# The first norm of a hybrid block as a pipeline in program order

## The chip, the cores and the metric

The kernel runs on one core of a Trainium2 chip. A core has a matrix engine (TensorE, PE in the profile), a vector engine (VectorE, DVE), an activation engine (ScalarE, ACT), a general engine (GpSimd, POOL) and a sync engine (SyncE, SP), from whose queue this kernel starts all its transfers. The metric is the device time of one execution in microseconds; less is better. Before the change it was 1269.47 us, the median of three runs (1269.19 to 1269.53).

## The reference

One layer of an encoder on 1024 tokens and 16 meta tokens of width 1024, in float32. What matters here is its beginning:

```python
h = jnp.concatenate([meta, x], axis=1)
u = rmsnorm(h, norm_mix)            # h * rsqrt(mean(h*h) + 1e-6) * norm_mix
z = jnp.einsum('bld,dn->bln', u, w_in)
a, q, k, v, r, lr, ga, gb = jnp.split(z, IN_SPLITS, axis=-1)
```

From these eight parts a pooling mixer and a chunked gated linear attention are computed, merged by sigmoid gates, projected and added to h; a second norm, a squared-ReLU MLP (1024 to 4096 to 1024) and a last norm follow.

## The kernel before, in words

Every product is made in split precision: an operand is stored as a rounded high part and a low part that holds the rest, and a product is the sum of three (high by high, high by low, low by high). The high part is an ACT copy, the low part a subtraction on DVE or POOL.

The function `start` (lines 513 to 573) makes the first norm and turns the result. The tokens are eight tiles of 128 rows. For a tile t, `layer_norm` (221) sums the squares of each row on ACT (226), takes the inverse root with two small ACT and four small DVE instructions (`inv_sqrt`, 199), and scales by the root and by norm_mix on DVE (228); norm_mix lies on all 128 partitions in `gB`, put there by a transfer that repeats the row 128 times (537). `turned` (502) transposes the normed tile on PE in two groups of four into two PSUM banks, and copies each bank three times: the high part into `TH` (ACT, 196), the low part into `TL` (DVE, 197) and the plain value into `ut` (ACT, 511). Tiles 0 to 3 are the first token half, 4 to 7 the second.

`v_tile(0, t)` (456) multiplies the turned tile by 272 weight columns, 256 value columns and 16 of a low-rank gate, in 24 PE instructions into one bank. Two copies leave the bank: the 16 columns on DVE into `lrtok` (470), then the 256 on ACT into `v` (474). `load_vw` (441) loads and splits these weights. `lr_turn` (476) transposes lrtok.

`Quarters` (285) makes the gate projections by a Strassen-like scheme of seven products P1 to P7 per pair of weight blocks, each 12 PE instructions. P1 and P2 take the first token half as it is; P5, P6, P7 and P4 take sums and differences of the transposed halves, which `differences` (588) makes out of `ut` (lines 580, 581 and 586). `prime` (334) makes the first four weight operands, P1 and P2 of two pairs; each `next(run)` in `start` issues one product. P2 adds to P1's bank, but only once ACT has copied P1 out of it (360). P5 is the first product after `differences`.

What sets the order: PE's instructions are issued in the order of the code (1449). SP, ACT, DVE and POOL are ordered by a planner, which takes what it expects to be ready and prefers what stands earlier in the code. Each engine then works strictly through its list, and waits for semaphores where an input or a buffer isn't free. In the code the products P1 and P2 of the first pair and `v_tile` of tile 0 stand ahead of the norm of tile 4, `v_tile` of tiles 1 to 3 between the tiles 5 to 7, and `v_tile` of tiles 4 to 7 in `differences`, behind the meta tokens (`v_tile(0, 8)`, 572).

PSUM: two banks `mm` for the value products, four banks `ms` for the transpositions, one double bank `sc` for P1 and P2.

Of the kernel before, what the change touches and what calls it, by code (L numbers as in the profile page):

```python
# [14 lines left out]
P = 128  # L15
# [88 lines left out]
def kernel(  # L104
# [81 lines left out]
    def f32(ap):  # L186
        return ap.bitcast(F32)
# [32 lines left out]

    def layer_norm(xt, u):

        rows = xt.shape[0]
        ss = ln_stat[ln_n[0] % 4][:rows]
        ln_n[0] += 1
        act.activation(u, xt, ACT.Square, accum_out=ss)
        rs = inv_sqrt(ss, 1, 1.0 / D)
        dve.scalar_tensor_tensor(u, xt, rs, gB[:rows], ALU.mult, ALU.mult)

    turn_n = [0]  # L230

# [206 lines left out]
    def halves():  # L438
        return [slice(h * HALF, (h + 1) * HALF) for h in range(2)]

    def load_vw(i):
        vw, n = S["vw"][i], 256 + 16 * (i == 0)
        for j in range(2):
            r = raw.load(w_cols(C_V + i * 256 + j * P), D).rearrange("p (k c) -> p k c", k=KT)
            c = slice(j * P, (j + 1) * P)
            act.activation(vw[:, 0, :, c], r, ACT.Copy)
            eng = pool if i else dve
            eng.tensor_tensor(vw[:, 1, :, c], r, f32(vw[:, 0, :, c]), ALU.subtract)
        if i == 0:
            r = S["lrraw"]  # L450
            act.activation(vw[:, 0, :, 256:], r, ACT.Copy)
            pool.tensor_tensor(vw[:, 1, :, 256:], r, f32(vw[:, 0, :, 256:]), ALU.subtract)

    vm = gB[32 : 32 + META, : 2 * 256]

    def v_tile(i, t):

        vw, w = S["vw"][i], 256 + 16 * (i == 0)
        if t == 8:
            half, at, n = 0, 0, META  # L460
        else:
            half, n = t // 4, P
            at = OFF[half] + (t % 4) * P
        b = bank("mm")[:n, :w]
        mm3(
            b, KT, lambda k: (TH[half][:, k, at : at + n], TL[half][:, k, at : at + n]),
            lambda k: (vw[:, 0, k], vw[:, 1, k]),
        )
        if i == 0:
            dve.tensor_copy(S["lrtok"][:n, t], b[:, 256:])  # L470
        if t == 8:
            act.activation(vm[:, i * 256 : i * 256 + 256], b[:, :256], ACT.Copy)
        else:
            act.activation(S["v"][i][:, t], b[:, :256], ACT.Copy)

    def lr_turn():
        b = bank("ms")
# [21 lines left out]
        lambda i, w, b, u: gate_result(i, w, b, u),  # L499
    )  # L500

    def turned(u, t):

        half, at = t // 4, OFF[t // 4] + (t % 4) * P
        for j in range(2):
            b = quad(bank("ms"))
            for i in range(4):
                pe.transpose(b[:, i], u[:, (4 * j + i) * P : (4 * j + i + 1) * P], ident)
            k = slice(4 * j, 4 * j + 4)
            split_from_psum(TH[half][:, k, at : at + P], TL[half][:, k, at : at + P], b)  # L510
            act.activation(S["ut"][half, j][:, :, (t % 4) * P : (t % 4 + 1) * P], b, ACT.Copy)

    def start():
        act.preload_act_table_set("natural_log_exp_and_others")
# [18 lines left out]
        S["vw"] = [right.push("vw0", [P, 2, KT, VP], F32R)]  # L533
        load = lambda t: nc.sync.dma_start(xs[:, t % 4], x[t * P : (t + 1) * P, :])
        load(0)
        nc.sync.dma_start(ident, ident_in)
        nc.sync.dma_start(gB, bcast(norm_mix))
        for t in (1, 2, 3):
            load(t)
        q.load(0, 0)  # L540
        m = lambda half, j: tuple(a[half][:, 4 * j : 4 * j + 4, OFF[half] : OFF[half] + HALF] for a in (TH, TL))
        q.x.update({"P1": m(0, 0), "P2": m(0, 1), "P3": m(1, 1)})
        run = S["gate_run"] = q.run()
        for t in range(8):
            if t < 4:
                layer_norm(xs[:, t % 4], us[:, t % 3])
                turned(us[:, t % 3], t)
                load(t + 4)
                if t == 0:
                    nc.sync.dma_start(S["lrraw"], w_in[:, C_LR : C_LR + 16].rearrange("(k p) c -> p k c", p=P))  # L550
                    load_vw(0)
                    q.load(1, 0)
                continue
            if t == 4:
                nc.sync.dma_start(xm, meta)
                q.load(0, 1)
                q.load(1, 1)
                nc.sync.dma_start(mf, masks)
                q.prime()
                next(run)  # L560
                next(run)
                v_tile(0, 0)
            layer_norm(xs[:, t % 4], us[:, t % 3])
            turned(us[:, t % 3], t)
            if t < 7:
                v_tile(0, t - 3)
            else:
                layer_norm(xm, um)
        next(run)
        transposed(um, 0, 0)  # L570
        next(run)
        v_tile(0, 8)
        pool.tensor_copy(mask, mf)
# [14 lines left out]
    def differences():  # L588

        b11, b21, b12, b22 = (0, 0), (0, 1), (1, 0), (1, 1)  # L590
        left.pop_to(S["left_x"])
        differ(b11, b12, b11)
        halved("P5", b11)
        differ(b12, b22, b12)
        differ(b22, b22, b11)
        halved("P6", b22)
        for t in range(4, 8):
            v_tile(0, t)
        lr_turn()
        right.pop_to(S["right_ut"][4])  # L600
        halved("P7", b12)
        differ(b21, b21, b22)
        right.pop_to(S["right_ut"][2])
        halved("P4", b21)
        right.pop_to(S["right_ut"][0])
# [884 lines left out]
```

## Time and profile before

| | before |
|---|---|
| median of three runs | 1269.47 us |
| profiled execution | 1271.45 us |
| its span in the trace | 1269.7 us |
| VectorE busy | 853.2 us |
| ScalarE busy | 625.2 us |
| GpSimd busy | 60.3 us |

The profiled execution is one run under the profiler; its span goes from the first to the last instruction on the chip. All times within the trace count from the span's start. A row of the timeline gives the start, the duration, the engine, the line, the operation, what it writes and reads, how many like it follow each other (x), and in brackets how long its engine had been idle before it and what it then waited for.

### The profile page before, as it was taken

How to read it: one execution, taken by the hardware profiler on the slowest of the kernel's cores; microseconds unless marked ns; L12 is line 12 of the kernel's file. 1: busy time of each engine (PE TensorE's matmuls, PEld its weight loads, DVE VectorE, ACT ScalarE, POOL GpSimd, SP SyncE). 2: the span in 40 equal slices, each digit the busy share in tenths (PEclk: the TensorE clock that was granted, in tenths of full speed). 3: DMA queues.
4: the chain of work that ended last, by engine and by line, in shares of the span. 5: the costliest groups of instructions: out<-in, count | busy, mean ns of one | idle time of the engine just before them, and what ended most of it. 6: DMA issues, size and time to landing. Idle time of an engine off the chain costs nothing.

```text
span 1269.7 us, 18153 instructions
## 1 busy us (share of the span) xinstructions
PE 1221.4 (96%) x6799; PEld 1003.4 (79%) x6799; DVE 853.2 (67%) x1403; ACT 625.2 (49%) x1101; POOL 60.3 (5%) x38
## 2 busy tenths in 40 slices
PE   3999999999999999899999999999999999999997
PEld 2888888888787877788878888888878788888775
DVE  6776667563355766842797766766764877887685
ACT  7567757431344664421565554544553444445444
POOL 0000000001000114510000000000000000000000
PEclk9999999999999999999999999999999999999999
DMA  9023334327210326860234444444469863332422
GB/s 261 1 67 108 113 95 143 115 67 231 84 35 10 95 93 205 275 239 34 84 116 158 162 146 149 157 150 149 160 221 373 275 230 100 95 97 92 166 92 83
DMA packets 143864, 175.41 MB, mean 138 GB/s; under 512 B 11008, under 2 KB 83472, under 8 KB 143776
## 3 DMA queue, kind: packets, MB, share of 16 engines
q1 hardware_dynamic: 143776, 174.25, 42.3%
q8 instruction: 53, 0.87, 0.3%
q14 instruction: 35, 0.29, 0.1%
HBM read 120.74 MB, written 53.48 MB: 137 GB/s over the span
## 4 chain that ended last, share of the span: by engine, by line
PE 86%; DVE 5%; ACT 3%; DMA 3%; issue 2%; POOL 1%; SPq 0%; DVEq 0%; ACTq 0%; POOLq 0%
PE b_mm L252 8%; PE b_mm L254 8%; PE b_mm L253 8%; PE b_o L253 8%; PE b_o L254 8%; PE b_o L252 8%; PE b_y L252 5%; PE b_y L254 5%; PE b_y L253 5%; PE b_z L252 3%; PE b_sc L252 3%; PE b_z L253 3%; PE b_sc L253 3%; PE b_sc L254 3%; PE b_z L254 3%
## 5 line engine op out<-in xcount | busy, mean ns | idle before, releaser
L252 PE MATMUL b_mm<-th,w1h 128*128 128x512 f32 (+1 forms) x240 | 86.9, 362 | 0.9 <-ACT w1h L75 0.9
L254 PE MATMUL b_mm<-th,w1l 128*128 128x512 f32 (+1 forms) x240 | 84.5, 352 | 0.7 <-DVE w1l L76 0.7
L253 PE MATMUL b_mm<-tl,w1h 128*128 128x512 f32 (+1 forms) x240 | 84.6, 352 | 0.0
L270 ACT ACTIVATE w1h<-raw 128x512 fp32r<-128x512 f32 x96 | 59.6, 623 | 45.1 <-PE b_sc L253 14.2
L252 PE MATMUL b_sc<-th,w1h 128*128 128x512 f32 x192 | 77.1, 402 | 1.8 <-ACT u2p L360 1.8
L252 PE MATMUL b_o<-w1h 128*128 128x512 f32 x192 | 75.3, 392 | 2.7 <-DVE h L1298 1.7
L253 PE MATMUL b_sc<-tl,w1h 128*128 128x512 f32 x192 | 76.2, 397 | 0.3 <-DVE tl L197 0.3
L253 PE MATMUL b_o<-w1l,w1h 128*128 128x512 f32 x192 | 75.0, 391 | 1.2 <-DVE w1l L271 1.2
L254 PE MATMUL b_sc<-th,w1l 128*128 128x512 f32 x192 | 76.2, 397 | 0.0
L254 PE MATMUL b_o<-w1h,w1l 128*128 128x512 f32 x192 | 75.0, 391 | 0.1
L271 DVE TENSOR_TENSOR w1l<-raw,w1h 128x512 fp32r<-128x512 f32 x96 | 65.6, 684 | 12.4 <-ACT w1h L270 12.4
L270 ACT ACTIVATE w1h<-fs 128x512 fp32r<-128x512 f32 x72 | 45.4, 630 | 49.9 <-PE b_y L253 34.4
L252 PE MATMUL b_z<-th,w1h 128*128 128x512 f32 x160 | 62.5, 391 | 0.8 <-DVE c L612 0.8
L253 PE MATMUL b_z<-tl,w1h 128*128 128x512 f32 x160 | 62.4, 390 | 0.4 <-DVE tl L1210 0.4
L254 PE MATMUL b_z<-th,w1l 128*128 128x512 f32 x160 | 62.3, 389 | 0.0
L271 DVE TENSOR_TENSOR w1l<-fs,w1h 128x512 fp32r<-128x512 f32 x72 | 49.3, 685 | 17.5 <-ACT w1h L270 17.5
L270 ACT ACTIVATE w1h<-bt 128x512 fp32r<-128x512 f32 x45 | 28.3, 630 | 57.1 <-issue 33.5
L1361 DVE TENSOR_TENSOR bt<-w,w 128x512 f32<-128x512 f32 x80 | 54.7, 684 | 2.4 <-DMA w<-in_w_ff_dram 2.4
L252 PEld LDWEIGHTS b_mm<-th,w1h 128*128 128x128 f32 x240 | 45.8, 191 | 10.1 <-issue 2.3
L254 PEld LDWEIGHTS b_mm<-th,w1l 128*128 128x128 f32 x240 | 45.9, 191 | 7.0 <-DVE w1l L76 1.0
L253 PE MATMUL b_o<-fxl,fxh 128*128 128x512 f32 x128 | 50.0, 391 | 0.7 <-DVE small L213 0.7
L252 PE MATMUL b_mm<-wo,th 128*128 128x512 f32 x128 | 50.7, 396 | 0.0
(334 smaller groups left out, 3396.4 us busy)
## 6 DMA issues: line engine op xcount, KB each, us to landing
hf_dram<-h SPq DMA_DIRECT2D x112, 256.0 KB, 2.1
raw<-hf_dram SPq DMA_DIRECT2D x112, 256.0 KB, 2.6
w<-in_w_ff_dram SPq DMA_DIRECT2D x64, 256.0 KB, 5.1
raw<-in_w_in_dram SPq DMA_DIRECT2D x24, 512.0 KB, 4.6
raw<-in_w_ff_dram SPq DMA_DIRECT2D x16, 512.0 KB, 4.1
rawx<-in_w_ff_dram SPq DMA_DIRECT2D x16, 512.0 KB, 4.2
xs<-in_x_dram SPq DMA_DIRECT2D x8, 512.0 KB, 6.3
rawx<-in_w_in_dram SPq DMA_DIRECT2D x8, 512.0 KB, 4.5
```

The source lines that it names most:

```text
L252: pe.matmul(ps, ah, bh, start=first and i == 0, stop=False, skip_group_check=more)
L253: pe.matmul(ps, ah, bl, start=False, stop=False, skip_group_check=more)
L254: pe.matmul(ps, al, bh, start=False, stop=last and i == n - 1, skip_group_check=more)
L270: act.activation(hi, a, ACT.Copy)
L271: dve.tensor_tensor(lo, a, f32(hi), ALU.subtract)
L1361: dve.tensor_tensor(bt, w, S["w2"][q[3:]][:, i], ALU.add if q[2] == "+" else ALU.subtract)
```

## The change

`start` becomes a software pipeline. The loop of tile t first issues the norm and the transpositions of tile t + 1, then the copies out of the banks of tile t (`taken`), the copies of the values of tile t - 1 (`leave`), and the value product of tile t. Within this loop ACT and DVE keep the order of the code, like PE (`manual_schedule`). The three copies of a bank are redistributed: both high parts on ACT, both low parts on DVE, of the plain values one on ACT and one on DVE.

norm_mix is loaded as one row of 4 KB and spread by two PE products with a column of ones, one for each half of `gB`; two DVE copies bring it from PSUM to `gB`, behind the inverse root of tile 0 and ahead of its scaling. The value weights are loaded ahead of x tiles 2 and 3; one half of their low part moves from DVE to POOL, and the 16 columns' low part from POOL to DVE. `prime` moves into the loop, behind the values of tile 4. All value products of the eight tiles come in the loop; the P1 and P2 products of the first two pairs all come behind it, and the norm of the meta tokens too. `differences` loses its four value products.

```diff
--- before.py
+++ after.py
@@ -220,12 +220,17 @@
 
     def layer_norm(xt, u):
 
+        scaled(xt, u, inv_rms(xt, u))
+
+    def inv_rms(xt, u):
         rows = xt.shape[0]
         ss = ln_stat[ln_n[0] % 4][:rows]
         ln_n[0] += 1
         act.activation(u, xt, ACT.Square, accum_out=ss)
-        rs = inv_sqrt(ss, 1, 1.0 / D)
-        dve.scalar_tensor_tensor(u, xt, rs, gB[:rows], ALU.mult, ALU.mult)
+        return inv_sqrt(ss, 1, 1.0 / D)
+
+    def scaled(xt, u, rs):
+        dve.scalar_tensor_tensor(u, xt, rs, gB[: xt.shape[0]], ALU.mult, ALU.mult)
 
     turn_n = [0]
 
@@ -438,22 +443,24 @@
     def halves():
         return [slice(h * HALF, (h + 1) * HALF) for h in range(2)]
 
-    def load_vw(i):
+    def fetch_vw(i):
+        return [raw.load(w_cols(C_V + i * 256 + j * P), D).rearrange("p (k c) -> p k c", k=KT) for j in range(2)]
+
+    def load_vw(i, raws=None):
         vw, n = S["vw"][i], 256 + 16 * (i == 0)
-        for j in range(2):
-            r = raw.load(w_cols(C_V + i * 256 + j * P), D).rearrange("p (k c) -> p k c", k=KT)
+        for j, r in enumerate(raws or fetch_vw(i)):
             c = slice(j * P, (j + 1) * P)
             act.activation(vw[:, 0, :, c], r, ACT.Copy)
-            eng = pool if i else dve
+            eng = pool if i or j else dve
             eng.tensor_tensor(vw[:, 1, :, c], r, f32(vw[:, 0, :, c]), ALU.subtract)
         if i == 0:
             r = S["lrraw"]
             act.activation(vw[:, 0, :, 256:], r, ACT.Copy)
-            pool.tensor_tensor(vw[:, 1, :, 256:], r, f32(vw[:, 0, :, 256:]), ALU.subtract)
+            dve.tensor_tensor(vw[:, 1, :, 256:], r, f32(vw[:, 0, :, 256:]), ALU.subtract)
 
     vm = gB[32 : 32 + META, : 2 * 256]
 
-    def v_tile(i, t):
+    def v_tile(i, t, later=False):
 
         vw, w = S["vw"][i], 256 + 16 * (i == 0)
         if t == 8:
@@ -466,12 +473,17 @@
             b, KT, lambda k: (TH[half][:, k, at : at + n], TL[half][:, k, at : at + n]),
             lambda k: (vw[:, 0, k], vw[:, 1, k]),
         )
-        if i == 0:
-            dve.tensor_copy(S["lrtok"][:n, t], b[:, 256:])
-        if t == 8:
-            act.activation(vm[:, i * 256 : i * 256 + 256], b[:, :256], ACT.Copy)
-        else:
-            act.activation(S["v"][i][:, t], b[:, :256], ACT.Copy)
+        def leave():
+            if i == 0:
+                dve.tensor_copy(S["lrtok"][:n, t], b[:, 256:])
+            if t == 8:
+                act.activation(vm[:, i * 256 : i * 256 + 256], b[:, :256], ACT.Copy)
+            else:
+                act.activation(S["v"][i][:, t], b[:, :256], ACT.Copy)
+
+        if later:
+            return leave
+        leave()
 
     def lr_turn():
         b = bank("ms")
@@ -499,16 +511,24 @@
         lambda i, w, b, u: gate_result(i, w, b, u),
     )
 
-    def turned(u, t):
+    def turned(u):
+        b = [quad(bank("ms")) for _ in range(2)]
+        for j in range(2):
+            for i in range(4):
+                pe.transpose(b[j][:, i], u[:, (4 * j + i) * P : (4 * j + i + 1) * P], ident)
+        return b
+
+    def taken(b, t):
 
         half, at = t // 4, OFF[t // 4] + (t % 4) * P
+        parts = [[a[half][:, 4 * j : 4 * j + 4, at : at + P] for a in (TH, TL)] for j in range(2)]
+        ut = [S["ut"][half, j][:, :, (t % 4) * P : (t % 4 + 1) * P] for j in range(2)]
         for j in range(2):
-            b = quad(bank("ms"))
-            for i in range(4):
-                pe.transpose(b[:, i], u[:, (4 * j + i) * P : (4 * j + i + 1) * P], ident)
-            k = slice(4 * j, 4 * j + 4)
-            split_from_psum(TH[half][:, k, at : at + P], TL[half][:, k, at : at + P], b)
-            act.activation(S["ut"][half, j][:, :, (t % 4) * P : (t % 4 + 1) * P], b, ACT.Copy)
+            act.activation(parts[j][0], b[j], ACT.Copy)
+        act.activation(ut[0], b[0], ACT.Copy)
+        for j in range(2):
+            dve.tensor_tensor(parts[j][1], b[j], f32(parts[j][0]), ALU.subtract)
+        dve.tensor_copy(ut[1], b[1])
 
     def start():
         act.preload_act_table_set("natural_log_exp_and_others")
@@ -533,41 +553,60 @@
         S["vw"] = [right.push("vw0", [P, 2, KT, VP], F32R)]
         load = lambda t: nc.sync.dma_start(xs[:, t % 4], x[t * P : (t + 1) * P, :])
         load(0)
+        nc.sync.dma_start(um[:1], norm_mix[None, :])
         nc.sync.dma_start(ident, ident_in)
-        nc.sync.dma_start(gB, bcast(norm_mix))
-        for t in (1, 2, 3):
-            load(t)
-        q.load(0, 0)
+        load(1)
+        raws = fetch_vw(0)
+        nc.sync.dma_start(S["lrraw"], w_in[:, C_LR : C_LR + 16].rearrange("(k p) c -> p k c", p=P))
+        load(2)
+        load(3)
         m = lambda half, j: tuple(a[half][:, 4 * j : 4 * j + 4, OFF[half] : OFF[half] + HALF] for a in (TH, TL))
         q.x.update({"P1": m(0, 0), "P2": m(0, 1), "P3": m(1, 1)})
         run = S["gate_run"] = q.run()
-        for t in range(8):
+        def norm(t):
+            x_, u = xs[:, t % 4], us[:, t % 3]
+            scaled(x_, u, inv_rms(x_, u))
             if t < 4:
-                layer_norm(xs[:, t % 4], us[:, t % 3])
-                turned(us[:, t % 3], t)
                 load(t + 4)
+            return turned(u)
+
+        with tc.manual_schedule(engines={mybir.EngineType.Activation, mybir.EngineType.DVE}):
+            dve.memset(xm[:1, :P], 1.0)
+            wide_g = []
+            for c in halves():
+                b = bank("mm")
+                pe.matmul(b, xm[:1, :P], um[:1, c], start=True, stop=True)
+                wide_g.append((b, c))
+            x_, u = xs[:, 0], us[:, 0]
+            rs = inv_rms(x_, u)
+            for b, c in wide_g:
+                dve.tensor_copy(gB[:, c], b)
+            scaled(x_, u, rs)
+            load(4)
+            b, leave = turned(u), None
+            for t in range(8):
+                new = norm(t + 1) if t < 7 else None
+                if t in (1, 2):
+                    q.load(t - 1, 0)
+                if t == 3:
+                    nc.sync.dma_start(xm, meta)
+                    q.load(0, 1)
+                    q.load(1, 1)
+                    nc.sync.dma_start(mf, masks)
                 if t == 0:
-                    nc.sync.dma_start(S["lrraw"], w_in[:, C_LR : C_LR + 16].rearrange("(k p) c -> p k c", p=P))
-                    load_vw(0)
-                    q.load(1, 0)
-                continue
-            if t == 4:
-                nc.sync.dma_start(xm, meta)
-                q.load(0, 1)
-                q.load(1, 1)
-                nc.sync.dma_start(mf, masks)
-                q.prime()
-                next(run)
-                next(run)
-                v_tile(0, 0)
-            layer_norm(xs[:, t % 4], us[:, t % 3])
-            turned(us[:, t % 3], t)
-            if t < 7:
-                v_tile(0, t - 3)
-            else:
-                layer_norm(xm, um)
+                    load_vw(0, raws)
+                taken(b, t)
+                if leave:
+                    leave()
+                if t == 5:
+                    q.prime()
+                b, leave = new, v_tile(0, t, True)
+            leave()
+        layer_norm(xm, um)
+        next(run)
         next(run)
         transposed(um, 0, 0)
+        next(run)
         next(run)
         v_tile(0, 8)
         pool.tensor_copy(mask, mf)
@@ -594,8 +633,6 @@
         differ(b12, b22, b12)
         differ(b22, b22, b11)
         halved("P6", b22)
-        for t in range(4, 8):
-            v_tile(0, t)
         lr_turn()
         right.pop_to(S["right_ut"][4])
         halved("P7", b12)
```

## The prediction

> **What bounds the kernel now.** I read the page first, then TensorE's stretches, then who it waited for at the head.
>
> ```profile
> PE 1221.4 (96%) x6799; PEld 1003.4 (79%) x6799; DVE 853.2 (67%) x1403; ACT 625.2 (49%) x1101; POOL 60.3 (5%) x38
> ```
>
> ```profile
> 0.00:27.20 27.20, 7.62 (x32) 1.00 0.97 284
> 8.50:15.00 6.50, 1.97 (x8) 1.00 1.14 327
> 27.20:75.80 48.60, 47.18 (x314) 1.00 0.05 12
> ```
>
> ```profile
> PE b_ms L508 <- DVE us L228: 14.3, 3, 8.5
> PE b_ms L508 <- DVE small L206: 5.2, 1, 5.2
> ```
>
> TensorE (PE) is busy 96% of the span; columns of the second fence are stretch, length, PE busy, clock, DMA share, GB/s. The large hole is the start: 7.62 us of work in 27.2, all of it transpositions, and two waits of 14.3 and 5.2 us for normed tiles. From 27.2 to 75.8 PE is full. So only the first 77 us can pay, by at most the 19.6 us idle there. After that PE is the bound, and what the head wins or loses reaches the end.
>
> **The change, part by part.** First the price of one norm (start, duration):
>
> ```profile
> 4.28 1.06 ACT L226 ACTIVATE us<-xs 128x1024 f32<-128x1024 f32 x1 [2.27 <-DMA xs<-in_x_dram]
> 5.24 0.19 ACT L226 ACTIVATION_READ_ACCUMULATOR us<-xs 128x1 f32 x1
> 5.53 0.29 ACT L205 ACTIVATE small<-small 128x1 f32<-128x1 f32 x1
> 5.85 0.20 ACT L207 ACTIVATE small<-small 128x1 f32<-128x1 f32 x1
> 6.09 0.22 DVE L209 SCALAR_TENSOR_TENSOR small<-small 128x1 f32<-128x1 f32 x1 [0.47 <-ACT small L207]
> 6.34 0.15 DVE L213 TENSOR_SCALAR small<-small 128x1 f32<-128x1 f32 x1
> 6.53 0.16 DVE L214 TENSOR_TENSOR small<-small 128x1 f32<-128x1 f32 x1
> 7.17 1.28 DVE L228 SCALAR_TENSOR_TENSOR us<-xs,small,gB 128x1024 f32<-128x1024 f32 x1 [0.48 <-DMA gB<-in_norm_mix_dram]
> ...
> 44.89 0.16 DVE L214 TENSOR_TENSOR small<-small 128x1 f32<-128x1 f32 x1
> 45.09 1.28 DVE L228 SCALAR_TENSOR_TENSOR us<-xs,small,gB 128x1024 f32<-128x1024 f32 x1
> 46.29 1.28 DVE L197 TENSOR_TENSOR tl<-b_ms,th 128x512 fp32r<-128x512 f32 x2
> ...
> 51.92 0.17 DVE L470 COPY lrtok<-b_mm 128x16 f32<-128x16 f32 x1 [1.51 <-PE b_mm L254]
> 52.13 0.38 ACT L474 ACTIVATE v<-b_mm 128x256 f32<-128x256 f32 x1 [1.08 <-DVE lrtok L470]
> 52.41 1.08 ACT L196 ACTIVATE th<-b_ms 128x512 fp32r<-128x512 f32 x2
> 53.03 1.29 DVE L197 TENSOR_TENSOR tl<-b_ms,th 128x512 fp32r<-128x512 f32 x2 [0.94 <-ACT th L196]
> 53.76 1.20 ACT L511 ACTIVATE ut<-b_ms 128x512 f32<-128x512 f32 x2 [0.27 <-DVE tl L197]
> ```
>
> The last five rows decide. ACT sat idle 1.08 us and took its copy of v only at 52.13, when DVE had finished the 16 columns of the same bank (51.92 + 0.17 = 52.09), though PE had been done at 51.9. Likewise ut started at 53.76, behind the first tl (53.03 + 0.68 = 53.71), though th was over at 53.49. Two readers of one PSUM bank go one after the other, in the order of the code. The Trainium skill, page "PSUM — Partial Sum Buffer", section "PSUM bank collisions raise a hardware error", says two engines must not be in one bank at once; the 1.08 us row agrees, and by it the third case below would not occur.
>
> *The loop.* Today the planner may put other work on ACT and DVE ahead of such a wait; the change fixes both to the order written. In tile t ACT does norm(t+1), th(t) twice, ut(t), v(t-1); DVE does norm(t+1), tl(t) twice, the other ut(t), lrtok(t-1). So v(t-1) waits for the lrtok that stands last on DVE, behind L228(t+1), and the Square of norm(t+2), queued behind v(t-1), waits too; everything waits for that norm. The ring, start to start: v to Square 0.28 (52.13 to 52.41); Square to accumulator 0.96; to Ln 0.29; to Exp 0.32; to L209 0.24; 0.25; 0.19; to L228 0.20 (44.89 to 45.09); to tl 1.20; tl to tl 0.60; tl to copy 0.60; copy to lrtok 0.60; to v 0.21. Sum 5.94 us a tile. No 512-column DVE copy from PSUM is shown; the lrtok row (0.17) and this one bound it below, a 512-column subtraction (0.68) stands beside it; in line it comes to 0.68:
>
> ```profile
> L937 DVE COPY S<-b_ms 128x128 f32<-128x128 f32 x2 | 0.6, 284 | 2.1 <-PE b_ms L933 2.1
> L448 POOL TENSOR_TENSOR vw<-raw,vw 128x1024 fp32r<-128x1024 f32 x2 | 4.8, 2414 | 77.8 <-ACT vw L446 77.8
> L896 PE MATMUL b_ms<-gB,wgu x8: 587/640/692, 335.7 to 449.5; 16*128 16x512 f32 x8
> ```
>
> (At 0.28 the ring is 0.4 shorter.) PE has less to do per tile:
>
> ```profile
> 48.60 0.37 PE L252 MATMUL b_mm<-vw,th 128*128 128x272 f32 x1
> 51.72 1.03 PE L508 MATMUL b_ms<-ident,us 128*128 128x128 f32 x8
> 52.51 0.48 PE L252 MATMUL b_sc<-th,w1h 128*128 128x512 f32 x1
> 56.51 0.51 PE L252 MATMUL b_sc<-th,w1h 128*128 128x512 f32 x1 [0.39 <-ACT u2p L360]
> 59.41 0.29 PE L252 MATMUL b_mm<-vw,th 128*16 128x272 f32 x1
> 62.40 0.29 PE L252 MATMUL b_mm<-vw,th 128*128 128x272 f32 x1
> 74.72 1.04 PE L483 MATMUL b_ms<-ident,lrtok 128*16 128x128 f32 x8
> 77.15 0.50 PE L252 MATMUL b_z<-P5h,w1h 128*128 128x512 f32 x1 [1.39 <-ACT gB L484]
> ```
>
> Value product 48.60 to 51.72 = 3.12, transpositions 0.79: 3.91 in 5.94. The loop is bound by the ACT–DVE ring, PE idle 2.0 a tile.
>
> *norm_mix by a product.* The 512 KB transfer goes; 4 KB and two one-row products come. Like L896 these take 0.6 to 1.3 (half clock) each, and PE is idle until 8.5 today. But the two copies stand behind L214 (done 6.69) and ahead of L228: 1.2, so L228(0) starts at 7.9 where it started at 7.17: 0.75 lost. Won: x(1), 0.59 MB behind x(0) at 327 GB/s, is there at 6.1, the value weights (1.05 MB, now ahead of x(2)) at 9.3, x(2) at 11.1.
>
> *First tiles.* Normed tile 0 at 9.2; its transpositions run slow:
>
> ```profile
> 8.51 1.97 PE L508 MATMUL b_ms<-ident,us 128*128 128x128 f32 x8 [8.51 <-DVE us L228]
> 21.63 1.17 ACT L270 ACTIVATE w1h<-rawx 128x512 fp32r<-128x512 f32 x2
> ```
>
> They end at 11.2. ACT has split the value weights by 10.6 (two Square-sized copies from 9.3), then does th, th, ut: Square(2) at 12.4. POOL's new half of the subtraction (2.41) ends at 12.8, the first value product starts at 13.1: nothing waits for POOL. The 16-column subtraction that DVE takes back is under 0.3, beside ACT's work; the later loads on SP's queue have 5 us or more of room.
>
> *Sum.* Square(7) at 12.4 + 5 x 5.94 + 2.2 = 44.3; the 2.2 are prime()'s four ACT splits (1.17 for two), now in line after tile 4. L228(7) 2.45 later, 46.7; transposed 48.8; product 6 to 51.9. th(7) and ut(7) wait for v(5) at 49.9, tl(7) from 51.9; product 7 ends at 55.5. Behind it stand two pairs P1, P2 (52.51 to 59.41: 6.9 each), the meta values 3.0, the lrtok transpositions (1.04 + about 0.6, bounds 0.3 and 1.3, as tile 8's lrtok is now last and may find DVE in a 1.2 us subtraction), and the 1.39 wait that stands before P5 today. P5 starts at 75.3; today 77.15: -1.8. The four products moved in front of lr_turn cost nothing twice, they only leave lines 597–598. DVE's work for P5 to P7 starts at 54, as today.
>
> *The clock.*
>
> ```profile
> 520.00:524.00 4.00, 2.96 (x14) 1.00 0.88 302
> 528.00:531.50 3.50, 1.64 (x6) 1.00 0.77 284
> 531.50:535.00 3.50, 3.50 (x10) 0.51 0.86 246
> ```
>
> After a stretch with PE half busy, 3.5 us ran at 0.51; after 74% busy it stayed at 1.00. In the loop PE is 66% busy, with stretches under half. A slow product there has 2.0 us of cover. Before transpositions 7, though, PE stands 4.2 us (product 5 ends at 43.8); what follows has no cover, and one or two such stretches at half speed cost 1.7 to 3.4. I take +1.1 between 0 and 3.4. The Trainium skill, page "TensorE: Matmul & The Clock Gate", section "Part 1: The HAM clock gate", asks for an idle window of 3.4 us; by that rule only the 4.2 us gap counts and the term is 0 or 1.7. The rows show that half busy is enough.
>
> Net -0.7: from the profiled 1271.45 (span 1269.7 and 1.75 around it) to 1270.75; the median of the runs is 1.98 lower, so **1268.8**.
>
> **Rivals.** *Uncoupled:* v doesn't wait for lrtok, as if fixed order did not bind there. The tile then takes PE's 3.91, five rings give 5 x 2.0 = 10 us: 1258.5. Against it the 1.08 us row. *Foreign work in the ring (slower):*
>
> ```profile
> 26.99 0.68 DVE L320 TENSOR_TENSOR fs<-raw 128x512 f32<-128x512 f32 x1
> ```
>
> Sums for P5 stood between norms before. Fixed order binds only the loop's own instructions; the planner may still fill DVE's 2 us holes, and where it puts such an operation between L228 and lrtok it lengthens the ring. Two sums, two differences, two splits (0.68 each) and the meta row's L228 (1.28) make 5.4 at most: 1274.2. It turns the sign once 0.7 lands on the ring, and is measurably slower from 3.2. *Clock at its dear end:* +3.4 in place of 1.1: 1271.1; with late value weights (+2) 1273.
>
> **How the numbers follow.** 0.2% is 2.5 us, about what a measurement can tell from no change. The sum as it stands: 0.58 (its own range 1266 to 1272.5), of which 0.12 faster, 0.38 same, 0.08 slower. Uncoupled 0.16, all faster. Foreign work 0.18, all slower. Clock with late weights 0.08: 0.02 same, 0.06 slower. Together faster 0.28, same 0.40, slower 0.32. The range 1262 to 1274.5 leaves out most of the uncoupled case and little else.
>
> **What would show it.** Right: Squares of tiles 3 to 6 some 5.9 us apart, ACT idle before each v with lrtok as releaser; PE idle 2 us before each set of transpositions; 4 us before the eighth; P5 near 76. Squares 4 us apart and P5 near 66 would prove the coupling wrong; L320 or L586 rows between L228 and lrtok would show the slower rival; a clock of 0.5 near 50 us the last one.

## The result and the profile after

The changed kernel takes 1271.10 us, median of twenty runs (1269.0 to 1273.0); twenty runs of the kernel before beside them gave 1270.69 (1269.2 to 1274.0). The ratio is 1.0002 with a 95% interval of 0.9995 to 1.0008: no change that can be measured. Forecast was 0.7 us less, called "same" as the likeliest.

Yet the beginning looks quite different. First ACT's timeline (start, duration, engine, line, operation; in brackets the idle time before and what ended it). Line 229 is the Square, 482 the copy of v, 478 the copy of lrtok.

```profile
13.38 1.06 ACT L229 ACTIVATE us<-xs 128x1024 f32<-128x1024 f32 x1
...
22.20 0.38 ACT L482 ACTIVATE v<-b_mm 128x256 f32<-128x256 f32 x1 [5.64 <-DVE lrtok L478]
22.48 1.05 ACT L229 ACTIVATE us<-xs 128x1024 f32<-128x1024 f32 x1
...
28.06 0.39 ACT L482 ACTIVATE v<-b_mm 128x256 f32<-128x256 f32 x1 [2.40 <-DVE lrtok L478]
28.34 1.05 ACT L229 ACTIVATE us<-xs 128x1024 f32<-128x1024 f32 x1
...
34.19 1.05 ACT L229 ACTIVATE us<-xs 128x1024 f32<-128x1024 f32 x1
...
40.04 1.05 ACT L229 ACTIVATE us<-xs 128x1024 f32<-128x1024 f32 x1
...
47.98 1.04 ACT L229 ACTIVATE us<-xs 128x1024 f32<-128x1024 f32 x1
```

Before each v ACT stands idle, and each time lrtok releases it. The Square behind v therefore comes every 5.85 us (22.48, 28.34, 34.19, 40.04). Now TensorE, its timeline and then its windows (window, length, PE busy, clock, DMA share, GB/s):

```profile
4.54 3.75 PE L578 MATMUL b_mm<-um,xm 1*128 1x512 f32 x4 [4.54 <-DMA um<-in_norm_mix_dram]
...
16.09 0.56 PE L258 MATMUL b_mm<-vw,th 128*128 128x272 f32 x1 [1.41 <-DVE vw L459]
...
17.00 0.43 PE L257 MATMUL b_mm<-vw,th 128*128 128x272 f32 x1
17.22 0.43 PE L258 MATMUL b_mm<-vw,th 128*128 128x272 f32 x1
...
38.00 1.06 PE L518 MATMUL b_ms<-ident,us 128*128 128x128 f32 x8 [1.76 <-DVE us L233]
...
52.01 1.33 PE L518 MATMUL b_ms<-ident,us 128*128 128x128 f32 x8 [4.07 <-DVE us L233]
...
80.82 0.50 PE L257 MATMUL b_z<-P5h,w1h 128*128 128x512 f32 x1 [1.17 <-ACT gB L496]
```

```profile
50.00:54.00 4.00, 1.99 (x12) 0.83 0.02 4
54.00:58.00 4.00, 4.00 (x27) 0.74 0.00 0
...
339.40:342.80 3.40, 3.40 (x17) 0.50 0.61 130
```

PE waits 1.76 us ahead of the transpositions of a tile and 4.07 ahead of the eighth; P5 starts at 80.82, 3.67 **later** than the 77.15 of before. So the rearrangement leaves the head longer, and still the end comes at the same time. Laid instruction by instruction beside before, PE is 3.67 us late at P5, 2.61 from 92 us on, 2.06 at 320 and 0.54 at 536. The last step lies at before's half-clock stretch of 531.5, where the change ran at full clock:

```profile
531.50:535.00 3.50, 2.75 (x12) 1.00 0.67 233
```

Two questions follow: where the gain of the head went, and whether a late head is always forgiven.

The head was lengthened ahead of the ring, too. VectorE's timeline, then GpSimd's:

```profile
8.33 0.69 DVE L583 COPY gB<-b_mm 128x512 f32<-128x512 f32 x1 [0.84 <-PE b_mm L578]
9.06 1.28 DVE L233 SCALAR_TENSOR_TENSOR us<-xs,small,gB 128x1024 f32<-128x1024 f32 x1
...
12.35 3.40 DVE L455 TENSOR_TENSOR vw<-raw,vw 128x1024 fp32r<-128x1024 f32 x1
```

```profile
11.92 2.74 POOL L455 TENSOR_TENSOR vw<-raw,vw 128x1024 fp32r<-128x1024 f32 x1 [11.09 <-ACT vw L453]
```

The second copy to `gB` waits for the second one-row product, so the first scaling starts at 9.06. VectorE's half of the subtraction takes 3.40 us, beside 2.74 of GpSimd's half. The first value product has one instruction at 14.11; the second waits 1.41 us for the low part of the weights and starts at 16.09. From 17.00 to 21.75 they follow each other every 0.226 us, those of the next product every 0.127: the first ran at half clock.

### The profile page after: what moved, and what is told of

It is laid out like the page before. It is cut to its first block, busy times and chain, and to the rows that moved or that the text cites. A ratio compares the mean times of both kernels' runs of the same rounds, so it can differ in the third digit from the quotient of the medians.

```text
span 1269.4 us, 18168 instructions
## 1 busy us (share of the span) xinstructions
PE 1224.0 (96%) x6803; PEld 1004.4 (79%) x6803; DVE 862.9 (68%) x1414; ACT 623.0 (49%) x1093; POOL 63.4 (5%) x38
## 4 chain that ended last, share of the span: by engine, by line
PE 85%; DVE 6%; ACT 3%; DMA 3%; issue 2%; POOL 1%; SPq 0%; DVEq 0%; ACTq 0%; POOLq 0%
PE b_mm L257 8%; PE b_mm L259 8%; PE b_o L258 8%; PE b_o L259 8%; PE b_o L257 8%; PE b_mm L258 8%; PE b_y L257 5%; PE b_y L259 5%; PE b_y L258 5%; PE b_z L258 3%; PE b_sc L257 3%; PE b_z L257 3%; PE b_z L259 3%; PE b_sc L258 3%; PE b_sc L259 3%
```

## The experiments

The theory after the result: *the fixed order on ACT holds the next Square behind v, and v waits for the last thing VectorE does for the tile (lrtok)*. Its rivals: that the slow beginning alone (norm_mix by a product, GpSimd's half, the clock) ate the gain; that fixed order as such, on either engine, costs; and that the ring doesn't matter because the end absorbs any shift of the head. "P5" below is the start of P5 in the one profiled run of a kernel; before has 77.15. Two profiles of the changed kernel differ by 0.96, so a difference under 1 us in this column shows nothing by itself.

| kernel | P5, us | time, us | before beside it | ratio, 95% interval |
|---|---|---|---|---|
| the change | 80.82 | 1271.10 | 1270.69 | 1.0002 (0.9995 to 1.0008) |
| the change, second set | 79.86 | 1270.75 | 1269.72 | 1.0005 (0.9996 to 1.0015) |
| v ahead of lrtok | 77.14 | 1265.24 | 1271.56 | 0.9958 (0.9944 to 0.9973) |
| both low halves on VectorE | 80.08 | 1269.99 | 1271.56 | 0.9989 (0.9981 to 0.9998) |
| norm_mix by transfer | 81.45 | 1272.95 | 1271.56 | 1.0013 (1.0004 to 1.0021) |
| no fixed order | 70.60 | 1262.65 | 1271.56 | 0.9933 (0.9921 to 0.9946) |
| before, padded | 81.05 | 1273.40 | 1270.96 | 1.0018 (1.0008 to 1.0028) |
| no fixed order, v first, halves on VectorE | 69.63 | 1260.04 | 1270.96 | 0.9918 (0.9904 to 0.9932) |
| fixed on ACT alone | 78.99 | 1272.49 | 1270.96 | 1.0009 (0.9998 to 1.0020) |
| fixed on VectorE alone | 72.28 | 1264.26 | 1270.96 | 0.9946 (0.9933 to 0.9960) |
| before, v ahead of lrtok | 77.21 | 1270.74 | 1269.79 | 1.0006 (0.9996 to 1.0015) |
| the combination, row first | 67.22 | 1258.36 | 1269.79 | 0.9906 (0.9891 to 0.9920) |
| the combination, columns late | 71.53 | 1261.05 | 1269.79 | 0.9929 (0.9915 to 0.9943) |

### v ahead of lrtok

```diff
         def leave():
-            if i == 0:
-                dve.tensor_copy(S["lrtok"][:n, t], b[:, 256:])
             if t == 8:
                 act.activation(vm[:, i * 256 : i * 256 + 256], b[:, :256], ACT.Copy)
             else:
                 act.activation(S["v"][i][:, t], b[:, :256], ACT.Copy)
+            if i == 0:
+                dve.tensor_copy(S["lrtok"][:n, t], b[:, 256:])
```

> The changed kernel with one thing turned round: in leave() ACT copies the 256 values first and DVE the 16 lrtok columns after it, so that ACT no longer stands behind DVE's last operation of the tile. Theory (the wait of v for lrtok makes the ring of 5.85 us a tile that the changed kernel's trace shows from its fourth to its seventh Square): Squares of tiles 3 to 6 then stand about 4.0 us apart, bound by PE's 3.9 and DVE's 3.8 us; the eighth Square comes near 40 instead of 48, P5 starts near 74 instead of 80.8, and as some of the 2.4 us of waits that vanished behind the head may come back, the time falls by 4 to 7 us (ratio 0.9945 to 0.997 to before). Rival (DVE's own chain of Exp, scaling and low parts sets the pace, whoever goes first): Squares stay above 5.5 us apart and the time stays within 1 us of the changed kernel.

Measured: 6.3 us faster than before (0.9958), P5 at 77.14. ACT's timeline of this kernel (line 480 is v here):

```profile
25.91 0.38 ACT L480 ACTIVATE v<-b_mm 128x256 f32<-128x256 f32 x1 [0.55 <-PE b_mm L259]
26.19 1.06 ACT L229 ACTIVATE us<-xs 128x1024 f32<-128x1024 f32 x1
...
30.14 0.38 ACT L480 ACTIVATE v<-b_mm 128x256 f32<-128x256 f32 x1 [0.78 <-PE b_mm L259]
30.42 1.05 ACT L229 ACTIVATE us<-xs 128x1024 f32<-128x1024 f32 x1
```

The releaser of v has changed from lrtok to TensorE, the wait has shrunk from 2.40 to 0.55, and Squares come every 4.0 to 4.5 us. One exchange of two lines takes the ring away. It leaves the beginning as it was (the second instruction of the first value product starts at 16.00, in the change at 16.09), so the slow beginning alone didn't eat the gain. P5 came later than expected, for two reasons that stand in the trace: VectorE's timeline shows the meta row's scaling taken ahead of tile 7's, and PE ran two windows in a row at half clock there.

```profile
44.56 1.27 DVE L233 SCALAR_TENSOR_TENSOR um<-xm,small,gB 16x1024 f32<-16x1024 f32 x1
45.76 1.27 DVE L233 SCALAR_TENSOR_TENSOR us<-xs,small,gB 128x1024 f32<-128x1024 f32 x1
```

```profile
46.00:50.00 4.00, 2.83 (x13) 0.50 0.02 4
50.00:54.00 4.00, 4.00 (x25) 0.67 0.00 0
```

That is the prediction's "foreign work" rival, at a price of 45.76 - 44.56 = 1.2 us, and in a kernel whose ring is gone.

P5 stands where it stands in before (77.14 and 77.15), and yet the time is 6.3 us less. The profiled runs themselves took 1267.68 and 1271.45, 3.8 apart, and that all lies behind P5: 1.1 us at 92 us, which the section on the padding takes up, and the rest mostly at 337.0 and 531.6, where before ran at half clock and this run didn't. The other 2.5 us are between this profiled run, which had its two slow windows in the head, and the median of its kernel.

### Both low halves on VectorE

```diff
-            eng = pool if i or j else dve
+            eng = pool if i else dve
```

> The changed kernel with both halves of the value weights' low part on DVE again, none on POOL. In the changed kernel's trace DVE's half took 3.40 us beside POOL's, against about 1.2 alone. Theory (DVE stood still while POOL worked on the same memory): both halves on DVE take 2.4 us together, the low parts of tile 0 start about 0.9 us earlier, and everything up to P5 moves by about 0.9 us; P5 near 79.9, the time 0 to 1 us lower. Rival (the 3.40 has another cause, such as the transfers under way): a half on DVE still takes over 2 us, and P5 comes 1 to 3 us later.

Measured: 0.9989, P5 0.74 earlier. The eighth Square begins at 46.48 in place of 47.98; behind it PE ran two windows at half clock where the change ran one, so that P5 shows only half of this. VectorE's timeline:

```profile
12.35 2.35 DVE L455 TENSOR_TENSOR vw<-raw,vw 128x1024 fp32r<-128x1024 f32 x2
```

Two halves on one engine take 2.35 us together; one half beside GpSimd's took 3.40. GpSimd's help cost a microsecond. In the changed kernel GpSimd's half ended at 11.92 + 2.74 = 14.66, and VectorE's at 15.75, 1.09 later, about one undisturbed half (2.35 / 2 = 1.17). By the Trainium skill, page "SBUF — State Buffer", section "SBUF: two separate sides", the two engines share one pair of ports as an exclusive lock, for a VectorE operation with two inputs too, and the loser waits for the whole instruction; the 3.40 agrees with that to 0.1 us. Who starts first decides: in the kernel with v ahead of lrtok VectorE's half started at 12.28 and GpSimd's at 12.29; there VectorE's took 1.22 and GpSimd's 3.42, and VectorE's next subtraction, that of the 16 columns, 2.44 in place of 0.28.

### norm_mix by the repeating transfer again

```diff
-        nc.sync.dma_start(um[:1], norm_mix[None, :])
         nc.sync.dma_start(ident, ident_in)
+        nc.sync.dma_start(gB, bcast(norm_mix))
...
-                pe.matmul(b, xm[:1, :P], um[:1, c], start=True, stop=True)
...
-                dve.tensor_copy(gB[:, c], b)
```

> The changed kernel with norm_mix spread by the repeating transfer again, in place of the two products and two copies. Theory (the product costs time here, as the first scaling starts at 9.06 instead of 7.17, but the transfer of 512 KB delays x and the value weights by about 3 us, on which ACT waited at 9.13 and 10.79): first scaling near 7.2, second copy of the value weights near 13.5, first value product no earlier; P5 between 0 and 2 us later, time within 0.2% of the changed kernel. Rival (the first scaling sets everything): P5 about 1.5 us earlier.

Measured: 1.0013, P5 0.63 later. Square(1) began at 9.46 and Square(2) at 15.44, where the change has 6.53 and 13.38: the transfer holds up what is loaded behind it. The first scaling came earlier, at 8.23 in place of 9.06. So the product may be worth a little, about 0.1%, though it delays the first scaling; but the intervals of the two kernels overlap and 0.63 is less than two profiles of one kernel differ by, so this isn't shown.

### No fixed order

```diff
-        with tc.manual_schedule(engines={mybir.EngineType.Activation, mybir.EngineType.DVE}):
+        if True:
```

> The changed kernel without the fixed order on ACT and DVE: the planner orders them as in the kernel before, all else is as changed. Theory (a planner can put the next Square ahead of a waiting v): ACT idles less before v, tiles come 4 to 5.5 us apart, P5 3 to 6 us earlier and the time 1 to 4 us lower than the changed kernel. Rival (the planner's own estimates order worse than the code): tiles over 6 us apart, and the time 1 to 5 us higher than the changed kernel.

Measured: 0.9933, 8.9 us less, P5 at 70.60, more than expected. ACT, then PE:

```profile
20.43 1.06 ACT L229 ACTIVATE us<-xs 128x1024 f32<-128x1024 f32 x1
...
23.07 0.37 ACT L482 ACTIVATE v<-b_mm 128x256 f32<-128x256 f32 x1
```

```profile
26.34 1.04 PE L518 MATMUL b_ms<-ident,us 128*128 128x128 f32 x8
...
39.46 1.03 PE L518 MATMUL b_ms<-ident,us 128*128 128x128 f32 x8
...
43.37 1.04 PE L518 MATMUL b_ms<-ident,us 128*128 128x128 f32 x8
```

The rows of PE carry no bracket: at these tiles it no longer waits, and a tile takes 39.46 to 43.37 = 3.91 us, the price that the prediction named for its "uncoupled" case. v still follows lrtok; but a Square, whose input has long been there, now goes first.

### Fixed on one engine alone

```diff
-        with tc.manual_schedule(engines={mybir.EngineType.Activation, mybir.EngineType.DVE}):
+        with tc.manual_schedule(engines={mybir.EngineType.Activation}):
```

(in the second kernel `mybir.EngineType.DVE` in its place.)

> The changed kernel with the order fixed on ACT alone; DVE is ordered by the planner. Theory (the Square queued on ACT behind v, which waits for DVE's lrtok, makes the ring; a free DVE may take lrtok ahead of its other work): some of the 9 us between the fixed and the free order comes back, Squares 4.5 to 5.9 us apart, time 1265 to 1270. Rival (DVE's fixed order alone is what costs): as the free order, 1262 to 1264.

> The changed kernel with the order fixed on DVE alone; ACT is ordered by the planner, which may put the next Square ahead of v. Theory (the ring needs both engines fixed): the Square no longer stands behind lrtok, Squares 4 to 4.5 us apart, time 1262 to 1266. Rival (DVE's order is what costs): near the changed kernel, 1268 to 1271.

Measured: fixed on ACT alone, 1.0009, nothing won; fixed on VectorE alone, 0.9946, most of what the free order brings. The first missed its expectation: I had thought that a free VectorE would take lrtok early and loosen the ring. ACT's timeline shows that it did for one tile and not for the next:

```profile
25.59 0.38 ACT L482 ACTIVATE v<-b_mm 128x256 f32<-128x256 f32 x1 [0.25 <-DVE lrtok L478]
25.87 1.05 ACT L229 ACTIVATE us<-xs 128x1024 f32<-128x1024 f32 x1
...
32.68 1.06 ACT L229 ACTIVATE um<-xm 16x1024 f32<-16x1024 f32 x1 [3.35 <-DVE us L233]
...
33.74 0.36 ACT L482 ACTIVATE v<-b_mm 128x256 f32<-128x256 f32 x1
34.01 1.04 ACT L229 ACTIVATE us<-xs 128x1024 f32<-128x1024 f32 x1
```

It is 8.14 us between these two Squares of tiles, longer than any in the change between tiles 3 and 6. Here ACT stood 3.35 us until VectorE had scaled the next tile, then took the meta row's Square, and v came behind that: whatever VectorE takes first, ACT stands still behind it. It is ACT's fixed order that costs, not fixed order as such. The theory recorded for the second kernel, that the ring needs both engines fixed, falls with the first: ACT's alone costs as much as both.

### v ahead of lrtok in the kernel before

```diff
-        if i == 0:
-            dve.tensor_copy(S["lrtok"][:n, t], b[:, 256:])
...
+        if i == 0:
+            dve.tensor_copy(S["lrtok"][:n, t], b[:, 256:])
```

> The kernel before with v copied ahead of lrtok, nothing else. Theory (the wait of v for lrtok costs only where ACT's order is fixed; before, the planner has other work for ACT and TensorE is full from 27 us on): no change, within 1.5 us of before, P5 within 0.5 us of 77.15. Rival (the wait costs wherever it stands): 1.5 us or more faster.

Measured: 1.0006 (0.9996 to 1.0015), P5 at 77.21. The exchange that brings 6 us in the change brings nothing here: of the 1.08 us wait that the prediction found in the kernel before, only the end was lrtok's. Before, v started 0.2 us after PE was done (52.13 and 51.9); with the exchange ACT still idles 0.92 us at this place, and PE ends it (line 472 is v here):

```profile
52.02 0.38 ACT L472 ACTIVATE v<-b_mm 128x256 f32<-128x256 f32 x1 [0.92 <-PE b_mm L254]
```

And PE was full there (47.18 of 48.60 us), so nobody waited for the 0.2. The order of the two readers is what the prediction took from this row, rightly; the length of the wait is not what the order costs.

### The kernel before, with P5 put off

```diff
+        b = bank("mm")
+        for k in range(16):
+            pe.matmul(b, TH[1][:, k % 8, :P], TH[1][:, k % 8], start=k == 0, stop=k == 15)
         lr_turn()
```

Sixteen products that nobody reads stand ahead of the lrtok transpositions.

> The kernel before, with 16 products of 512 columns ahead of lr_turn whose result nobody reads (added work of 16 x 0.23 = 3.7 us on TensorE; ACT and DVE get nothing). Theory (a later P5 lets DVE and ACT run ahead, so that waits behind it vanish: in the changed kernel P5 came 3.7 us late and 0.95 us of that was gone 15 us later): P5 starts 3.7 us later, near 80.8, and the wait for L612 near 92 is gone; the time rises by 2 to 3 us, not by 3.7. Rival (what was made up behind P5 in the changed kernel belongs to its own order or to the clock): the time rises by 3.5 us or more.

Measured: P5 3.90 later, the time 2.4 us more (1.0018, that is 1.0 to 3.6). PE's waits between 77 and 120 us (engine, line, what it waited for; total, times, longest), first of the kernel before, then padded:

```profile
PE b_z L252 <- ACT gB L484: 1.4, 1, 1.4
PE b_z L252 <- DVE c L612: 0.8, 1, 0.8
```

```profile
PE b_z L252 <- ACT gB L484: 0.7, 1, 0.7
```

Who comes late to P5 finds less to wait for: the 0.8 us for VectorE's work behind it is gone, and 0.7 of the wait ahead of it. That second wait lies ahead of P5 and is already in its 81.05; the first is what P5's shift doesn't show. So a late P5 can be partly forgiven, some 1.5 of 3.9 us in the medians (0.3 to 2.9 by the interval), of which the trace shows 1.1 at this wait.

The change doesn't have the 0.8 us wait behind P5 either, but not because it comes late: none of its variants has it, and in those without a fixed order on ACT P5 is 4.9 to 9.9 us early (from 72.28, fixed on VectorE alone, to 67.22, row first). The cause can be read in VectorE's timeline of before:

```profile
89.41 0.69 DVE L320 TENSOR_TENSOR fs<-raw 128x512 f32<-128x512 f32 x1 [1.69 <-DMA raw<-in_w_in_dram]
```

VectorE had this sum ahead of the work that PE waited for, and stood 1.69 us until its weights had landed. Padded, the same sum starts at 89.47, and the late PE no longer notices. In the change VectorE has the sum at 93.94, behind the result that frees PE's bank (93.34), and waits for no transfer there. So the change wins 1.1 us here, whether its head is early or late. Why the planner places the sum otherwise isn't shown.

### The pieces together

The combination takes off the fixed order, puts v first and leaves both halves on VectorE. On it, two changes of SP's order were tried: the norm_mix row ahead of x tile 0, and the 16 columns' transfer behind x tiles 2 and 3.

```diff
+        nc.sync.dma_start(um[:1], norm_mix[None, :])
         load(0)
-        nc.sync.dma_start(um[:1], norm_mix[None, :])
```

```diff
-        nc.sync.dma_start(S["lrraw"], w_in[:, C_LR : C_LR + 16].rearrange("(k p) c -> p k c", p=P))
         load(2)
         load(3)
+        nc.sync.dma_start(S["lrraw"], w_in[:, C_LR : C_LR + 16].rearrange("(k p) c -> p k c", p=P))
```

> The changed kernel without the fixed order on ACT and DVE, with v copied ahead of lrtok and with both halves of the value weights' low part on DVE: the three changes that paid alone. Theory (each takes away a wait of its own): as the free order already brings tiles 3.9 us apart, which is TensorE's own work, the swap adds little; DVE's 3.4 us operation beside POOL goes, so the first product starts about 1 us earlier; P5 near 69.5, the time 0 to 1.5 us below that of the free order alone (1261 to 1262.7). Rival (the planner puts other work into what is freed): within 1 us of it, or above.

> The free order with swap and DVE's low parts (e6_free_swap_dve), the 4 KB row of norm_mix loaded ahead of x's first tile instead of behind it. In that kernel TensorE waited for the row until 4.54 and the spreading products ran to 8.3, after which came the second copy and the first scaling. Theory (the row sets the first scaling): products from about 3, second copy up to 1.5 us earlier, P5 0.5 to 1.5 us earlier, time up to 1.5 us lower. Rival (the second tile's x and the value weights, landed at 7.6 and 11.0, set the start): P5 within 0.5 us, same time.

> The free order with swap and DVE's low parts (e6_free_swap_dve), the transfer of the 16 gate columns issued behind x tiles 2 and 3 instead of ahead of them. In that kernel its issue held SP's queue for 3.58 us, and x tile 2 came at 12.6. Theory (the issue of many small pieces blocks what is behind it): tile 2's Square starts 1 to 2 us earlier and tile 0's value product not over 1 us later; P5 0 to 1 us earlier. Rival (the queue was full whoever stood there): the same stall shows on the next issue, the columns come later, and P5 is 0 to 2 us later.

Measured: the combination 0.9918, with the row first 0.9906 (11.4 us less than before, the fastest of all), with the columns late 0.9929. The combination's P5 came where it was expected; its step beyond the free order alone (0.9933) lies within the two intervals. PE's row of the kernel with the row first:

```profile
2.33 3.75 PE L578 MATMUL b_mm<-um,xm 1*128 1x512 f32 x4 [2.33 <-DMA um<-in_norm_mix_dram]
```

The row lands at 2.33 in place of 4.54, and P5 at 67.22 is 2.41 ahead of the combination's 69.63. The columns had been moved because SP stood on their issue; SP's timeline of the combination, then with the columns late:

```profile
3.91 3.58 SPq L560 DMA_DIRECT2D lrraw<-in_w_in_dram  x1
```

```profile
3.82 4.58 SPq L554 DMA_DIRECT2D xs<-in_x_dram  x2
8.45 0.43 SPq L562 DMA_DIRECT2D lrraw<-in_w_in_dram  x1
```

The stall stays, and whoever stands there has it: it isn't the columns' own. They are now issued at 8.45 in place of 3.91, and P5 comes 1.9 later. The third tile's transpositions already start 1.1 late (22.56 and 21.43); behind them PE ran one window at half clock (23.67 to 27.08) that the combination didn't have. So nothing was won, and the times (1261.05 and 1260.04) can't be told apart. The row first came 2.41 ahead, more than the 0.5 to 1.5 expected; its time and the combination's have overlapping intervals too.

### The change, a second time

The same kernel again, unchanged.

> The changed kernel as it is, a second time, since in its trace P5 came 3.67 us late and the span ended 0.3 us early, and 1.5 us of that lay at 531 to 535 us, where the trace of before ran one stretch at half clock and this one didn't. Theory (such stretches come and go from run to run, the head does not): P5 again within 0.5 us of 80.8, half-clock stretches behind P5 at another set of places, span up to 3.5 us away from 1269.4, and the time within 1.5 us of before. Rival (the change itself keeps the clock up behind the head): the same places as in its first trace, span within 0.3 us.

Measured: 1.0005 (0.9996 to 1.0015); P5 0.96 earlier, more than the 0.5 allowed, so the head comes and goes too. 0.91 of it stands at the v of tile 0 already (21.29 in place of 22.20): the second instruction of the first value product starts at 15.63 in place of 16.09, and part of this product ran at full clock, its instructions 0.13 us apart at 16.5. For the time, the clock behind P5 counts as well. In this run PE ran none of its windows behind P5 at half clock until near the end, where before had two (one of them at 531.5) and the first profile of the change one (at 339.4). PE's windows of this run, and its timeline, ahead of that of before at the same place:

```profile
528.00:531.50 3.50, 1.50 (x5) 1.00 0.79 276
531.50:535.00 3.50, 3.50 (x17) 1.00 0.80 250
```

```profile
529.25 0.50 PE L257 MATMUL b_mm<-yg,w1h 128*128 128x512 f32 x1 [1.50 <-ACT w1h L75]
...
530.74 0.50 PE L259 MATMUL b_mm<-yg,w1l 128*128 128x512 f32 x1 [0.75 <-DVE w1l L76]
```

```profile
529.10 0.50 PE L252 MATMUL b_mm<-yg,w1h 128*128 128x512 f32 x1 [1.51 <-ACT w1h L75]
...
530.59 0.50 PE L254 MATMUL b_mm<-yg,w1l 128*128 128x512 f32 x1 [0.76 <-DVE w1l L76]
...
531.62 0.63 PE L252 MATMUL b_mm<-yg,w1h 128*128 128x512 f32 x1
```

The same products wait 1.50 and 0.75 us in the one, 1.51 and 0.76 in the other; behind them the one runs at full clock, the other 3.4 us at half. Each such stretch costs about 3.4 / 2 = 1.7 us. By this estimate one or two more or fewer in a run would make 1.7 to 3.4 of the 4 to 5 us by which runs of one kernel differ here; the runs without a profile can't show how many they had.

## Why the prediction was right, and where it wasn't

**The result and its mechanism: right.** The forecast said that the pipeline would be bound by the ring of ACT and VectorE, not by PE, and that little would come out. The ring: 5.94 forecast, 5.85 measured, and the VectorE copy of a bank came to 0.68 (eight of them take 5.4), the value that was chosen between bounds:

```profile
L531 DVE COPY ut<-b_ms 128x512 f32<-128x512 f32 x8 | 5.4, 681 | 0.0
```

The gap ahead of the eighth transpositions: 4.2 forecast, 4.07. Square(3) to Square(7): 25.96 forecast, 47.98 - 22.48 = 25.50. The exchange of v and lrtok, the free order and the order fixed on one engine show that the ring was the cause, and that without it the rearrangement brings about what its rival "uncoupled" priced: 10 us of head there, and 80.82 - 70.60 = 10.2 between the P5 of the change and that without fixed order. Of these, 8.6 arise between the transpositions of tile 3 (26.29 and 26.34) and of tile 7 (52.01 and 43.37), the rest behind, where the change ran one window at half clock and the other none. That the two numbers meet so closely is in part chance; with the second profile of the change it is 9.3. The 1.08 us that the prediction set against this rival was PE's wait but for 0.2; what spoke against it was the order of the readers.

**The beginning: wrong by 4.1 us.** Square(3) was forecast at 12.4 + 5.94 = 18.3 and came at 22.48. Three terms were mis-sized:

- The second copy of `gB` was put at 6.69 + 0.6, behind two products that were said to be ready. They weren't: 4.54 for the row and 3.75 for its products, so the scaling came at 9.06, not 7.9. The load of one row is short, but it stood behind x tile 0; the kernel with the row first shows that.
- "Nothing waits for POOL" fell. The second half of the weights landed so late that its copy ended at 10.79 + 1.06 = 11.85, where 10.6 was assumed (by the prediction's own row, two copies of 1.06 from 9.3 end at 11.3 or so); POOL's half ended at 14.66, not 12.8; and VectorE's half, assumed at one undisturbed price, took 3.40. But for its first instruction, the first value product started at 16.09, not 13.1.
- "A slow product there has 2.0 us of cover" fell for the first one. It ran at half clock for 5.7 us in place of 3.1, and as it started 3 us late, v waited for it and not for the ring.

**The clock: right in size, wrong in its rule.** One half-clock stretch fell behind the 4.07 us gap, 1.7 us where 1.1 was taken. But "half busy is enough" doesn't hold as a rule: the same waits at 529 us were followed by half clock in one run and by full clock in another. Nor does the rule of an idle window alone: the gap ahead of that stretch in before was 1.51 us. In all fourteen profiles PE's clock changes only at whole multiples of 3.413 us from its first rise. Counted in these windows, the two waits fall into one in before (528.18 to 531.59, PE busy 1.73 of 3.41 us) and into two in the second profile of the change (2.38 and 2.20 of 3.41). The Trainium skill, page "TensorE: Matmul & The Clock Gate", section "Part 1: The HAM clock gate", also says that the 3.4 us window runs freely, without regard to the kernel's start; that would let equal gaps end differently, and these two runs agree with it. The busy share alone doesn't decide either: the half-clock window at 339.39 in the change followed one in which PE was busy for 2.52 of 3.41 us. What a window needs to stay at full clock remains open.

**"What the head wins or loses reaches the end": not one for one.** P5 came 4.4 us later than the 76.4 of the forecast (75.3 and 1.1 for the clock), and in the two profiles 3.7 and 2.7 later than before; by this step the time should have been about 3 us more. It was 0.4 and 1.0 more. 1.1 of the difference is the wait at 92 us that the change doesn't have. The rest stays open in the medians, whose intervals reach up to 1.0 and 1.9 us. In the pair of profiles it is mostly the half-clock stretch that before had at 531.6; but a single profile is no average: before with v ahead of lrtok has its P5 at 77.21, and its span is 1266.8 where that of before is 1269.7. A gain reached the end whole: without fixed order P5 was 6.6 us earlier and the time 8.9 less, and 1.1 of the 2.3 on top is the same wait. So the forecast of 0.7 less came out within the error from a cost in the head that was under-estimated and a gain behind it that was not foreseen. In this the number is luck; the ring is not.

**The rivals.** *Uncoupled* was wrong for the change, by its every v row, and right as a price. *Foreign work in the ring* didn't come about in the change: VectorE took the meta row's scaling at 46.09 and two sums at 27.94, both in its holes between lrtok and the next scaling; with prime()'s splits behind it, the first held up tile 7's root by about 0.2 us. *Clock at its dear end with late weights* was half right: the weights were late, by 3 us rather than 2, and the time stayed.

## What to carry to other kernels

Before you fix an engine's order by hand, look for the instruction in it that waits for another engine's last step, and for what is queued behind it: here one copy of 0.38 us held back the next tile by 1.4 to 1.9 us, tile after tile (5.85 against the 4.0 to 4.5 with v first). Where two engines read one PSUM bank, put first in the code the one whose queue is the critical one; but the same exchange was worth nothing in the kernel before, where PE was full, so price a wait by who is late behind it, and by what would end it if this releaser were gone. And before a GpSimd half is set beside a VectorE half, read what the VectorE instruction beside it takes.

## What the runs showed of the hardware

- A one-row float32 product of 512 columns is two PE instructions here, and two such products took 3.75 us at the head (four instructions, 0.94 each): 1.88 a product, more than the 0.6 to 1.3 that the prediction allowed.
- A VectorE subtraction of 128 x 1024 took 3.40 us when GpSimd's had started 0.43 us ahead of it (2.74), and 1.17 without it; when it started 0.01 us ahead of GpSimd's it took 1.22, and GpSimd's 3.42.
- SP stood 3.58 us on one issue, or 4.58 on the two that took its place, at the same moment of the program.
- The half-clock stretches of PE come and go between runs behind the same waits, by estimate 1.7 us each; all changes of PE's clock in one profile lie whole multiples of 3.413 us apart.
